# Weights of the second mixer split ahead of time, during the first MLP

## The chip, the cores and the metric

The kernel runs on one core of one Trainium2 chip. The metric is the device time of one execution in microseconds, the median of several runs. A core has TensorE (matrix products, with loads of the stationary operand listed apart), VectorE, ScalarE, GpSimd, and SyncE, which here issues nearly all DMAs. In the profile they are PE and PEld, DVE, ACT, POOL and SP. Each engine takes its own instructions in order and waits on semaphores for the others.

## The reference

The reference is one step of a decoder trunk of two layers in float32, for 1024 prompt tokens and 8 decode tokens together (T = 1032 columns), with a model dimension of 1024. Layer 0 has a hybrid mixer (gated delta rule and retention), layer 1 a Mamba-2 state-space mixer; each is followed by a squared-ReLU MLP with 4096 hidden features:

```python
h = rms_norm(x, norm_mix[layer])
out = mixer(h)                       # hybrid_mixer, then ssd_mixer
x = x + out
h = rms_norm(x, norm_mlp[layer])
x = x + einsum('blf,fd->bld', relu(einsum('bld,df->blf', h, w1)) ** 2, w2)
```

The second mixer starts with one projection of the normalised tokens:

```python
proj = einsum('bld,de->ble', h, w_in)          # w_in [1024, 5152]
z, xbc, dt_raw = split_last(proj, SSM_IN_SIZES)  # 2048, 3072, 32 columns
xbc = silu(causal_conv(xbc, conv_w, conv_b))
```

then runs a chunked scan over the tokens in four groups of heads, gates the result with silu(z), normalises it by group, and projects it back. The norm's weight per feature, norm_mix[1], can be multiplied into the rows of w_in; the norm's factor per token is applied to the product.

## The kernel before

**Exact parts.** A float32 product is made of three faster products. Each operand is split into two exact parts, a high one, which is the operand rounded by a cast to the type float32r, and a low one, the operand minus the high part. `mm3` (lines 148 to 152) adds whi·xhi, whi·xlo and wlo·xhi into one PSUM bank. The residual stream lies in SBUF as eight pairs of tiles xh, xl of [128, 1032]. Tokens are taken in three pieces of 344 columns.

**Weights.** `load_w` (lines 132 to 146) prepares 128 x 512 weights: a DMA on SyncE's queue brings them into a tile `raw` (three buffers, L136); GpSimd multiplies them by the norm's weight where there is one (L140); ScalarE casts the high part (L144); VectorE, or GpSimd for the down and output projections, subtracts to get the low part (L145). The parts have six buffers `hl`, that is three pairs. `load_half` calls it for half of an m-tile (128 output features by 512 of the 1024 inputs).

**Projections.** `products` (lines 165 to 175) makes an m-tile: for each of the two halves, three pieces of tokens by four k-tiles by three products, 36 products on one pair of parts. `gemm_units` evicts the three PSUM banks by a function that the caller gives. `gemm_flush` (lines 207 to 222) multiplies a block of up to eight k-tiles into all eight m-tiles of the model dimension.

**First MLP.** `mlp` (lines 1210 to 1325) makes 32 hidden m-tiles with `up`; after every fourth, `down` adds the block before into the residual's eight accumulators. `up` evicts through VectorE, ScalarE and GpSimd (L1225 to L1228), `down` by one VectorE addition (L1236).

**Second mixer.** Its 40 m-tiles of w_in lie in memory as `wis`, ten to a group of heads: four of x, one of B, one of C, four of the gate z. `ssm_setup` makes the narrow projection of dt and the first m-tile (number 4). In `ssm_mixers`, `conv_tile` and `gate` make the others; their evictions are L1451 (into the convolution's input sxc) and L1476 (into z). Between them runs `ssd_group`, the scan of a group: decays E (L1621 to L1629), the tokens scaled by dt, xdt (L1600), the scores sc (L1613), the state S, and the decode step with its state tiles dS (L1710 to L1731). The output projection's first block starts while the last group ends.

**Order.** The code emits the pieces of scan and projections in turn; a planner then sets each engine's order from these priorities, its own cost model and the buffers that are free at its modelled time. So a load is issued well before the product that needs it, but on each engine the order is fixed, and an instruction that waits holds all that stand behind it. On SyncE's queue the weight loads stand between the loads of the decode states (L1710), of the convolution states (L1458) and the stores of the new ones (L1468, L1469).

Of the kernel before, what the change touches and what calls it, by code (L numbers as in the profile page):

```python
# [18 lines left out]
P = 128  # L19
T = 1032                     # 1024 prompt tokens, then 8 decode tokens  # L20
# [4 lines left out]
KT = 8                       # k-tiles of the model dimension  # L25
WN = 384                     # tokens of a group of a narrow projection
CH = 128                     # mixer chunk
# the tokens in nines of 128, the last of which overlaps
# [3 lines left out]
HID = 32                     # hidden m-tiles of the MLP  # L32
PAST = 8192

# columns of the packed per-feature vectors
# [9 lines left out]
# order of the hybrid projection's m-tiles (first column of each)  # L45
# [14 lines left out]
# blocks of the output projections: the first packed column's k-tile, the mixer outputs  # L60
# [4 lines left out]
BS = 8                       # diagonal blocks that are inverted row by row  # L65
MASK_STEPS = [8, 16]         # doubling steps on whole chunks, with masks
BLOCK_STEPS = [32, 64]       # and on the blocks themselves
# [6 lines left out]
# columns of the retention's constants  # L74
# [9 lines left out]
class Pools:  # L84
    """A mixer's two pools: what the output projection's first block needs or reuses, and the rest."""
# [10 lines left out]
class Kern:  # L96
# [35 lines left out]
    def load_w(self, src, n, normw=None, lo_eng=None, dst=None, norm_eng=None):  # L132
        """src [128, n] of a packed weight unit -> exact float32r high and low parts."""
# [19 lines left out]

    def load_half(self, src, kh, M, normw):
        return self.load_w(src[:, kh * 4 * M:(kh + 1) * 4 * M], 4 * M, normw[:, kh * 4:kh * 4 + 4])

    def narrow(self, ps, w, x, k):
        """A k-tile of a projection of M <= 32 columns, in float32: ps[32 n:32 n + M, i] its token WN * n + i; the
        array takes the three groups of tokens side by side."""
        M = w.shape[1]  # L160
        for n in range(3):
            c = slice(n * WN, min(T, n * WN + WN))
            self.nc.tensor.matmul(ps[32 * n:32 * n + M, 0:c.stop - c.start], lhsT=w, rhs=x[:, c], start=k == 0, stop=k == KT - 1)

    def products(self, src, M, normw, pss):
        """The products of an m-tile over the model dimension; yields after every sixth."""
# [10 lines left out]
    def others(self):  # L177
        """The banks of the small products, for an m-tile."""
        return [self.pm(), self.ps2(), self.ps2()]

    def gemm_units(self, src, M, normw, evict, other=False):
        """One m-tile over the model dimension; evict(n, psum [M, 344]). other: in the banks of the small products.

        Yields after every sixth of the products; a pending rstd is worked out between them. self.first: the
        tile's psum, where its products are there already."""
# [21 lines left out]
    def gemm_flush(self, src, parts, evict):  # L207
        """A block of k-tiles into all 8 m-tiles; src(m) the packed weights [128, 128 * k-tiles]."""
# [16 lines left out]
    def split_piece(self, m, n, src, ssq, tp):  # L225
        """src [128, 344] fp32 becomes the residual's piece (m, n); its squares go to ssq."""
# [16 lines left out]
    def rsqrt(self, out, src):  # L243
        """out = (src) ** -0.5 for a small tile."""
# [7 lines left out]
    def rstd_from(self):  # L252
        """rstd_bc[:, t] = (sum_p ssq[p, t] / 1024 + eps) ** -0.5 on every partition; ssq lies where rstd_bc does."""
# [22 lines left out]
    def spread_end(self, pb, r, n):  # L276
        """pb[p, i] = r[128 - n + i] on every partition."""
        self.nc.tensor.matmul(pb[:, 0:n], lhsT=r.to_broadcast([P, P]), rhs=self.ident[:, P - n:P], start=True, stop=True)

    def spread(self, pb, rs):  # L280
        """pb[p, c * 128 + i] = rs[i, c] on every partition, from rs's two exact float32r parts."""
# [14 lines left out]
    def load_x(self, gp):  # L296
        """The tokens, as exact parts; their rstd; and the narrow projection, not yet scaled by it."""
# [25 lines left out]
        def square(m):  # L323
            """x[m]'s squares; those of four tiles are added up."""
# [49 lines left out]
    def softplus(self, out, x, tp, tag, bufs=None):  # L374
        """log1p(exp(x)) = max(x, 0) + 2 atanh(u / (2 + u)), u = exp(-|x|)."""
# [19 lines left out]
    def conv_silu(self, out, xc, st, wcol, bcol, tp):  # L395
        """Depthwise causal conv over the tokens of one 128-feature tile, then silu.

        xc [128, 3 + 1032] has three zero columns ahead; st [128, 3, 8] the decode rows;
        wcol(i) the tap halved, bcol the bias halved (or None)."""
# [16 lines left out]
    def silu2(self, x, scale, tp):  # L416
        """x (1 + tanh(scale x)) in place, in two halves."""
# [39 lines left out]
    def load_mixed(self, k, raw, hi, lo):  # L457
        """A spilled mixer output [128, 1024] and its decode columns, as exact parts."""
# [7 lines left out]
    def out_first(self, name, c0, parts, stage):  # L466
        """The first k-tiles of an output projection, with the residual, go to memory."""
# [12 lines left out]
    def hyb_mixers(self, gp):  # L480
# [34 lines left out]
        def ret(t, rr, vv, gg):  # L515
            for i in range(2):
# [3 lines left out]
                for q in range(4):          # the halves of each head's features change places  # L520
# [25 lines left out]
        def step():  # L546
            """Emits a sixth of a projection (and the end of the one before)."""
# [6 lines left out]
        def project(n):  # L554
            """Emits the projections up to tile n."""
# [6 lines left out]
        def weave(mix, need, rate):  # L562
            """Emits a mixer's pieces with `rate` sixths of a projection after each."""
# [16 lines left out]
        # the output projection's first block fills in while the last mixers finish  # L580
# [22 lines left out]
    def gdn_setup(self, gp, ba):  # L603
# [14 lines left out]
        gnh = gp.tile([P, 5], F32, name="gnh")     # norm weights of the gated outputs, halved  # L618
# [4 lines left out]
        # beta and decay: [8, T] -> token-major [128, 9, 8]  # L623
# [35 lines left out]
        # rows of the cumulated decay, as exact float32r parts stacked on the contraction  # L659
# [19 lines left out]
    def gdn_head(self, gp, h, feat, st):  # L679
# [10 lines left out]
        def bc(x, n=4):      # [128, n] -> [128, n, 128]  # L690
            return x.unsqueeze(2).to_broadcast([P, n, 128])

        def b3(x, n=4):      # [128, 128] -> [128, n, 128]
# [7 lines left out]
        for bi in range(2):  # L701
# [33 lines left out]
            # decay, transposed: DT[j, c, i] = exp(min(G_i - G_j, mask))  # L735
# [19 lines left out]
            # the diagonal blocks of the transposed factor, [block's row, chunk, row i]  # L755
# [5 lines left out]
        # their inverses: every row of a block needs the block's entries, lb[p, chunk, i, k] = L[block of p, i, k]  # L761
# [24 lines left out]
        # X = (I + L)^-1 by block doubling, two chunks at a time; XT its transpose  # L786
        units = [(B[bi], slice(2 * i, 2 * i + 2)) for bi in range(2) for i in range(2)]
        # (a step changes the columns of each 2b-block's upper right quarter alone, from its first b columns of X)
        for b in MASK_STEPS:
            def q4(x, half):      # [128, 2, 128] -> [128, 2, blocks, b], a half of each block's columns  # L790
                return x.rearrange("p c (n t b) -> p c n t b", t=2, b=b)[:, :, :, half, :]

            def c4(x):            # [128, 128] psum columns -> [128, 2, blocks, b]
# [60 lines left out]
        # the recurrence over the chunks  # L854
# [933 lines left out]
def pack(inp):  # L1788
# [3 lines left out]
    d = {}  # L1792
# [93 lines left out]
```

## Time and profile before

| | |
|---|---|
| runs | 3256.97, 3253.94, 3255.11 us; median 3255.11 |
| span of the profiled execution, first to last instruction | 3239.5 us |
| that execution's own time | not shown apart from its span |
| busy: TensorE, VectorE, ScalarE, GpSimd | 3086.4, 1740.3, 896.2, 1241.3 us |
| DMA | 202.13 MB, mean 62 GB/s |

A row of a group reads: line, engine, operation, output<-inputs by the program's names, shapes, count | busy time, mean ns of one | idle time of the engine just before them, and what ended it. A row of a window reads: start and end, length, then the busy time and count of PE, PEld, DVE, ACT and POOL, the clock that TensorE was granted (1.00 is full), the busy share of the DMA engines and GB/s. In a row of waits the instruction on the left waited for the one on the right. Matmuls overlap in the pipeline, so a single one's length is not its distance to the next.

### The profile page before, as it was taken

To read this page: it belongs to the slowest core of one execution; us is meant where nothing else is said; L and a number is where in the kernel's file an instruction comes from. 1 tells how busy PE (TensorE), PEld (TensorE's weight loads), DVE (VectorE), ACT (ScalarE), POOL (GpSimd) and SP (SyncE) were. 2 spreads that over 40 slices of the span, in tenths; PEclk is the share of its full clock that TensorE was granted. 3 is DMA by queue.
4 is the path that set the end of the run, shared out by engine and by line. 5 is a ranking of instruction groups with operands and counts; after the bars stand their busy time and mean duration, and the time that the engine had idled before them with its cause. 6 is when DMAs were issued, how large, how long until landed. Compare 5 with 4: busy or idle time off the path is not lost. (4 is left out here: it accounts for less than half of the span.)

```text
span 3239.5 us, 49390 instructions
## 1 busy us (share of the span) xinstructions
PE 3086.4 (95%) x19566; PEld 2929.6 (90%) x19566; DVE 1740.3 (54%) x3201; ACT 896.2 (28%) x1828; POOL 1241.3 (38%) x1234
## 2 busy tenths in 40 slices
PE   7989998989999999999999999999899999999998
PEld 6888888879999999999987788887899999999998
DVE  7664667464333333337886785967635333333334
ACT  3222221223111111114444444354213111111112
POOL 4232324155333323225355555444625332332324
PEclk9899999889999999999998898998899999999999
DMA  3011103142111111111111111222431111111112
GB/s 123 20 47 54 47 26 112 55 168 64 46 46 47 49 46 46 48 48 40 55 56 58 69 62 43 82 69 79 157 140 43 46 47 49 46 46 50 46 46 72
DMA packets 102326, 202.13 MB, mean 62 GB/s; under 512 B 12624, under 2 KB 27728, under 8 KB 102096
## 3 DMA queue, kind: packets, MB, share of 16 engines
q1 hardware_dynamic: 94800, 173.82, 16.7%
q0 software_dynamic: 7296, 25.17, 2.0%
q8 instruction: 154, 2.52, 0.3%
q14 instruction: 76, 0.62, 0.1%
HBM read 157.94 MB, written 38.89 MB: 61 GB/s over the span
## 5 line engine op out<-in xcount | busy, mean ns | idle before, releaser
L150 PE MATMUL pg<-xh,whi 128*128 128x344 f32 x3072 | 1020.7, 332 | 10.2 <-DVE sxc L1451 6.5
L152 PE MATMUL pg<-xh,wlo 128*128 128x344 f32 x3072 | 1012.9, 330 | 2.8 <-DVE wlo L145 2.8
L151 PE MATMUL pg<-xl,whi 128*128 128x344 f32 x3072 | 1009.0, 328 | 0.0
L150 PEld LDWEIGHTS pg<-xh,whi 128*128 128x128 f32 x3072 | 593.0, 193 | 27.7 <-issue 8.8
L152 PEld LDWEIGHTS pg<-xh,wlo 128*128 128x128 f32 x3072 | 592.8, 193 | 12.7 <-issue 5.2
L144 ACT CAST whi<-raw 128x512 fp32r<-128x512 f32 (+2 forms) x443 | 271.0, 612 | 1191.5 <-PE pg L151 723.9
L151 PEld LDWEIGHTS pg<-xl,whi 128*128 128x128 f32 x3072 | 592.3, 193 | 8.8 <-issue 5.8
L140 POOL TENSOR_TENSOR raw<-raw,vec 128x512 f32<-128x512 f32 x264 | 300.7, 1139 | 589.9 <-DMA raw<-w 339.7
L151 PE MATMUL pg<-alo,whi 128*128 128x344 f32 (+2 forms) x1476 | 472.4, 320 | 0.0
L152 PE MATMUL pg<-ahi,wlo 128*128 128x344 f32 (+2 forms) x1476 | 472.3, 320 | 0.0
L150 PE MATMUL pg<-ahi,whi 128*128 128x344 f32 (+2 forms) x1476 | 471.6, 319 | 0.0
L1236 DVE TENSOR_TENSOR acc<-acc,pg 128x344 f32<-128x344 f32 x360 | 182.8, 511 | 385.4 <-PE pg L152 385.4
L145 POOL TENSOR_TENSOR wlo<-raw,whi 128x512 fp32r<-128x512 f32 (+2 forms) x179 | 223.7, 1251 | 327.7 <-ACT whi L144 326.6
L145 DVE TENSOR_TENSOR wlo<-raw,whi 128x512 fp32r<-128x512 f32 x264 | 209.6, 794 | 193.3 <-ACT whi L144 172.2
L1227 POOL TENSOR_TENSOR r<-r 128x344 f32<-128x344 f32 x192 | 145.9, 760 | 387.6 <-ACT ahi L1226 338.5
L152 PEld LDWEIGHTS pg<-ahi,wlo 128*128 128x128 f32 x1476 | 277.6, 188 | 0.0
L150 PEld LDWEIGHTS pg<-ahi,whi 128*128 128x128 f32 x1476 | 277.5, 188 | 0.0
L151 PEld LDWEIGHTS pg<-alo,whi 128*128 128x128 f32 x1476 | 277.3, 188 | 0.0
L1228 DVE TENSOR_TENSOR alo<-r,ahi 128x344 fp32r<-128x344 f32 x192 | 135.6, 707 | 253.8 <-POOL r L1227 253.8
L1226 ACT ACTIVATE ahi<-r 128x344 fp32r<-128x344 f32 x192 | 94.5, 492 | 338.5 <-DVE r L1225 338.5
L1225 DVE SCALAR_TENSOR_TENSOR r<-pg,rstd_bc 128x344 f32<-128x344 f32 x186 | 94.8, 510 | 76.9 <-PE pg L152 75.6
L150 PE MATMUL pg<-mhi,whi 128*128 128x344 f32 x408 | 131.3, 322 | 4.1 <-DVE acc L1342 4.1
(534 smaller groups left out, 4422.9 us busy)
## 6 DMA issues: line engine op xcount, KB each, us to landing
raw<-w SPq DMA_DIRECT2D x256, 256.0 KB, 2.6
raw<-wis SPq DMA_DIRECT2D x80, 256.0 KB, 2.6
raw<-wih SPq DMA_DIRECT2D x56, 256.0 KB, 2.6
mraw<-spill SPq DMA_DIRECT2D x17, 512.0 KB, 4.1
accd<-ost SPq DMA_DIRECT2D x48, 172.0 KB, 2.1
acc<-accd SPq DMA_DIRECT2D x16, 516.0 KB, 6.9
dS<-sstate SPq DMA_DIRECT2D x32, 256.0 KB, 3.5
o_sssm<-dS POOLq DMA_DIRECT2D x32, 256.0 KB, 2.4
```

The source lines that it names most:

```text
L140: (norm_eng or nc.gpsimd).tensor_tensor(out=r3, in0=r3, in1=normw.unsqueeze(2).to_broadcast([P, k, n // k]), op=ALU.mult)
L144: nc.scalar.copy(hi[:, :n], raw[:, :n])
L145: (lo_eng or nc.vector).tensor_tensor(out=lo[:, :n], in0=raw[:, :n], in1=hi[:, :n].bitcast(F32), op=ALU.subtract)
L150: t.matmul(ps, lhsT=whi, rhs=xhi, start=start, stop=False)
L151: t.matmul(ps, lhsT=whi, rhs=xlo, start=False, stop=False)
L152: t.matmul(ps, lhsT=wlo, rhs=xhi, start=False, stop=stop)
L1225: nc.vector.scalar_tensor_tensor(out=r, in0=ps, scalar=0.0, in1=self.rstd_bc[:, s], op0=ALU.max, op1=ALU.mult)
L1226: nc.scalar.activation(hi[:, s], r, AF.Square)
L1227: nc.gpsimd.tensor_tensor(out=r, in0=r, in1=r, op=ALU.mult)
L1228: nc.vector.tensor_tensor(out=lo[:, s], in0=r, in1=hi[:, s].bitcast(F32), op=ALU.subtract)
L1236: nc.vector.tensor_tensor(out=s, in0=s, in1=ps, op=ALU.add)
```

## The change

A new generator `presplit` walks through the second mixer's 80 weight halves. For each it loads the weights into a tile of its own, multiplies by the norm's weight on GpSimd, casts on ScalarE and subtracts on VectorE, the same arithmetic as before, and stores both parts in a scratch buffer in device memory (40 tiles of [128, 4, 512], 1 MB each). The first MLP takes one step of it after each `up` and after the first seven m-tiles of each `down`, so all 80 are emitted before the last `down`. The second mixer passes the m-tile's number instead of its weights, and `load_half` then loads the two parts from the scratch buffer straight into an `hl` pair. The dt projection's weights (`wdt`), the other projections and the second MLP are as before. The MLP's pool holds six more tiles of 2 KB per partition. Comments are also taken out of the file, which shifts line numbers.

```diff
+    def presplit(self, tp):
+        nc, I = self.nc, self.I
+        normw = self.V("mix1", 0, 8)
+        for i in range(40):
+            for kh in range(2):
+                raw = tp.tile([P, 512], F32, tag="praw", name="praw", bufs=2)
+                nc.sync.dma_start(raw, I["wis"][i][:, kh * 512:kh * 512 + 512])
+                r3 = raw.rearrange("p (k c) -> p k c", k=4)
+                nc.gpsimd.tensor_tensor(out=r3, in0=r3, in1=normw[:, kh * 4:kh * 4 + 4].unsqueeze(2).to_broadcast([P, 4, 128]), op=ALU.mult)
+                hi, lo = [tp.tile([P, 512], F32R, tag="phl", name=nm, bufs=4) for nm in ("phi", "plo")]
+                nc.scalar.copy(hi, raw)
+                nc.vector.tensor_tensor(out=lo, in0=raw, in1=hi.bitcast(F32), op=ALU.subtract)
+                for s, x in enumerate((hi, lo)):
+                    nc.sync.dma_start(self.split[i][:, kh * 2 + s], x.bitcast(F32))
+                yield
+
     def load_half(self, src, kh, M, normw):
+        if isinstance(src, int):
+            hl = [self.wp.tile([P, 512], F32R, tag="hl", name=nm, bufs=6) for nm in ("whi", "wlo")]
+            for s, x in enumerate(hl):
+                self.nc.sync.dma_start(x.bitcast(F32), self.split[src][:, kh * 2 + s])
+            return hl
...
+            pre = iter(()) if last else self.presplit(tp)
             def up(t):
...
                 self.gemm_tile(I["w1"][l, t], 128, normw, ev, t == 1)
+                next(pre, None)
             def down(b):
...
-                for _ in self.gemm_flush(lambda m: I["w2"][l, b, m], [parts.pop(k) for k in ks], ev):
-                    pass
+                for m, _ in enumerate(self.gemm_flush(lambda m: I["w2"][l, b, m], [parts.pop(k) for k in ks], ev)):
+                    if m < 7:
+                        next(pre, None)
...
                 down(HID // 4 - 1)
+                for _ in pre:
+                    pass
...
-        for u, _ in enumerate(self.products(I["wis"][4], 128, normw, self.first)):
+        for u, _ in enumerate(self.products(4, 128, normw, self.first)):
...
-            self.gemm_tile(I["wis"][ti // 4 * 10 + ti % 4 if ti < 16 else ti % 4 * 10 + ti // 4], 128, normw, ev)
+            self.gemm_tile(ti // 4 * 10 + ti % 4 if ti < 16 else ti % 4 * 10 + ti // 4, 128, normw, ev)
...
-            self.gemm_tile(I["wis"][g * 10 + 6 + i], 128, normw, ev)
+            self.gemm_tile(g * 10 + 6 + i, 128, normw, ev)
...
+        sp = ctx.enter_context(tc.tile_pool(name="split", bufs=1, space=bass.MemoryType.DRAM))
+        k.split = [sp.tile([P, 4, 512], F32, name=f"split{i}") for i in range(40)]
```

## The prediction

> **What bounds the kernel now.** I read the page first, for engine shares and the slices in time; then two windows, the second mixer's projections (1489 to 2270 us) and the first MLP (790 to 1480 us).
>
> ```profile
> span 3239.5 us, 49390 instructions
> PE 3086.4 (95%) x19566; PEld 2929.6 (90%) x19566; DVE 1740.3 (54%) x3201; ACT 896.2 (28%) x1828; POOL 1241.3 (38%) x1234
> ```
> ```profile
> core 0: us, PE busy (x) PEld busy (x) DVE busy (x) ACT busy (x) POOL busy (x), PEclk, DMA share, GB/s
> 1489.00:2270.00 781.00, 731.26 (x4406) 650.22 (x4405) 597.71 (x955) 347.66 (x792) 379.63 (x341) 0.92 0.18 63
> 790.00:1480.00 690.00, 690.00 (x4387) 690.00 (x4386) 245.59 (x438) 130.03 (x236) 217.85 (x219) 1.00 0.15 47
> ```
>
> TensorE is the bound everywhere, but the two stages differ. In the MLP it has no idle time and the full clock, and every other engine is under 36% busy. In the mixer it is idle for 781 - 731.3 = 49.7 us, and its granted clock is 0.92, which costs about 731.3 x 0.08 = 58.5 us. So 108 us is the most that the mixer can give. VectorE there is 77% busy. The next view is who waits there (1480 to 2290 us); the numbers are the total in us, how often, and the longest.
>
> ```profile
> PE pm L1621 <- DVE xdt L1600: 14.0, 8, 3.0
> PE pm L1621 <- DVE sc L1613: 13.0, 5, 3.4
> PE pg L150 <- DVE sxc L1451: 6.5, 4, 2.7
> ...
> PE pg L152 <- DVE wlo L145: 2.8, 4, 1.7
> PE ps L1648 <- DVE x L1650: 2.2, 3, 1.0
> ...
> PE pg L150 <- ACT whi L144: 1.3, 2, 0.7
> ```
>
> Almost all of TensorE's idle time ends with a VectorE instruction. Here is one of the eight waits for xdt, with VectorE's instructions ahead of it (start, duration).
>
> ```profile
> 1640.23 0.50 PE L1621 MATMUL pm<-sgrow,ssel 64*128 64x256 f32 x2 [2.73 <-DVE xdt L1600]
> ```
> ```profile
> 1636.36 1.78 DVE L145 TENSOR_TENSOR wlo<-raw,whi 128x512 fp32r<-128x512 f32 x1
> 1638.06 0.67 DVE L1731 TENSOR_REDUCE dy<-dpr 128x4 f32<-128x512 f32 x1
> 1638.66 0.92 DVE L1451 TENSOR_TENSOR sxc<-pg,rstd_bc 128x344 f32<-128x344 f32 x2
> 1639.51 0.68 DVE L1600 TENSOR_TENSOR xdt<-pm,dt 128x512 f32<-128x512 f32 x1
> ```
>
> VectorE works without a pause, and the weights' subtraction (L145) stands in that queue. In the timeline all eight waits for xdt, and the three for x at L1650, have an L145 in the run-up like this one.
>
> **What the change removes from the mixer.** Each of its 80 weight halves loses three instructions.
>
> ```profile
> L140 POOL TENSOR_TENSOR raw<-raw,vec 128x512 f32<-128x512 f32 x80 | 98.3, 1229 | 134.3 <-DMA raw<-wis 104.5 <-DVE sxc L1451 12.4 <-DVE z L1476 10.0
> L145 DVE TENSOR_TENSOR wlo<-raw,whi 128x512 fp32r<-128x512 f32 x80 | 78.6, 983 | 13.3 <-PE pg L152 11.8 <-ACT whi L144 1.2
> ...
> L144 ACT CAST whi<-raw 128x512 fp32r<-128x512 f32 x85 | 52.6, 619 | 99.1 <-PE pg L151 41.6 <-issue 30.8 <-POOL raw L140 13.3
> ```
>
> Busy time falls by 98 us on GpSimd, 79 on VectorE (598 to about 519), and 80 x 0.619 = 50 on ScalarE. None of that is path time itself; what counts is the idle of TensorE behind it.
> - Waits for xdt, 14.0 us: each has one L145 of mean 0.98 us in front, so 8 x 0.98 = 7.9 us goes. Bounds: 0, if the next instruction in the queue has to wait for something else anyway, and 14.0. I take 7.9, since the queue shown has no idle in it.
> - Waits for x at L1650, 2.2 us over three: L145 is longer than the mean wait of 0.73, so all 2.2.
> - Waits for wlo and whi, 2.8 + 1.3 = 4.1 us: the instructions are gone; a late DMA could take their place (below). I take 4.1.
> - The waits for sc (13.0), sxc (6.5) and the others stay.
>
> That is 14.2 us of idle time, out of 20.3 in these groups. The second term is the clock. These are six stretches of low clock in the mixer that start with or just behind such a wait, and, last, one that starts with the longest wait for sc (3.4 us). The columns are those of the windows above:
>
> ```profile
> 1640.00:1646.00 6.00, 5.76 (x21) 4.21 (x21) 6.00 (x8) 4.33 (x14) 4.03 (x3) 0.72 0.01 4
> 1678.00:1690.00 12.00, 11.52 (x44) 9.04 (x45) 10.74 (x14) 9.48 (x25) 5.57 (x6) 0.72 0.09 32
> 1742.00:1758.00 16.00, 15.19 (x54) 12.95 (x55) 8.62 (x11) 9.21 (x25) 9.63 (x6) 0.57 0.13 48
> 1782.00:1794.00 12.00, 11.35 (x40) 9.61 (x41) 7.23 (x8) 9.52 (x26) 7.14 (x6) 0.58 0.08 23
> 2170.00:2178.00 8.00, 8.00 (x49) 7.00 (x48) 2.55 (x4) 4.65 (x10) 2.48 (x1) 0.79 0.01 2
> 2238.00:2246.00 8.00, 7.51 (x32) 6.01 (x32) 5.31 (x9) 5.97 (x17) 3.49 (x3) 0.79 0.29 98
> 1998.00:2022.00 24.00, 21.10 (x82) 18.29 (x84) 11.70 (x20) 9.50 (x23) 11.57 (x10) 0.57 0.09 33
> ```
> The second stretch starts with this wait:
>
> ```profile
> 1678.48 0.50 PE L1621 MATMUL pm<-sgrow,ssel 64*128 64x256 f32 x2 [1.98 <-DVE xdt L1600]
> ```
>
> Busy time x (1 - clock) of the first six is 1.6 + 3.2 + 6.5 + 4.8 + 1.7 + 1.6 = 19.4 us. I let as much of it go as of the idle that starts it, 14.2 / 20.3 = 0.70: 13.6 us (bounds 0 and 19.4).
>
> The Trainium skill ("TensorE: Matmul & The Clock Gate", section "Why this matters for your kernels") says that the clock falls back when TensorE idles for more than about 3 us between bursts. By that rule no wait that L145 lengthens is long enough, the second term is 0, and the time is 3240.9; this trace disagrees, since 1.98 us of idle at 1678.48 stands ahead of 12 us at 0.72.
>
> **What it adds to the first MLP.** Eighty units of one load (L140's kind of 256 KB), one GpSimd multiplication, one ScalarE cast, one VectorE subtraction, two stores of 256 KB. The first row prices a load, the second is the nearest to a store; the third is the time SyncE takes for an issue.
>
> ```profile
> raw<-wis SPq DMA_DIRECT2D x80, 256.0 KB, 2.6
> ...
> o_sssm<-dS POOLq DMA_DIRECT2D x32, 256.0 KB, 2.4
> ```
> ```profile
> L136 SPq DMA_DIRECT2D raw<-w x256: 327/328/377, 758.9 to 3181.4; - x128
> ```
> ```profile
> L140 POOL TENSOR_TENSOR raw<-raw,vec 128x512 f32<-128x512 f32 x57 | 60.3, 1057 | 168.3 <-DMA raw<-w 163.9 <-DVE acc L1236 4.4
> ```
> ```profile
> L144 ACT CAST whi<-raw 128x512 fp32r<-128x512 f32 x122 | 75.7, 620 | 385.5 <-PE pg L151 204.8 <-PE pg L152 136.3 <-POOL raw L140 40.6
> ```
> ```profile
> L145 DVE TENSOR_TENSOR wlo<-raw,whi x79: 669/692/2412, 1498.6 to 2264.3; 128x512 fp32r<-128x512 f32 x79
> ```
>
> GpSimd gets 80 x 1.057 = 85 us (218 to 303 of 690), ScalarE 80 x 0.62 = 50 (130 to 180), VectorE 80 x 0.69 = 55, at worst 80 x 2.41 = 193 (246 to 301, at most 439). SyncE issues 240 more DMAs, 240 x 0.328 = 79 us; they move 80 x 3 x 256 KB = 63 MB, some 91 GB/s on top of the 47. TensorE's uninterrupted 690 us hide all of it: cost 0. Without that cover the three instructions of a unit would be 2.37 us on the path, 190 us in all.
>
> The store is where a wait is added: SyncE waits for the cast, then for the subtraction, and the MLP's own weight loads (L136) are queued behind it; GpSimd's and ScalarE's weight work waits for those, and TensorE for that. The cast L144 shows the slack: of 385.5 us idle before it, 341 ended when TensorE released a buffer, so weights sit ready, three halves ahead. A half lasts 36 products; the MLP's 4387 in 690 us make 5.7 us. A store must hold SyncE for more than two halves, 11 us, before TensorE feels it; lower bound 0, upper bound one such miss at each of the eight down projections, about 3 us each, 24 us. I take 0.
>
> **What is moved.** The mixer's 80 loads become 160, straight into the product's buffers: 160 x 0.328 = 52 us of SyncE's 781. The wait for a free buffer moves from ScalarE (41.6 us on L144) to SyncE; the raw data no longer waits ahead of it. Cost 0 if the three pairs of buffers suffice.
>
> Sum: 14.2 + 13.6 = 27.8 us, 0.85%. The profiled span of 3239.5 becomes 3211.7. No time of that execution beside its span is shown; the median of the runs, 3255.1, lies 15.6 above it, which I leave as it is: 3255.1 - 27.8 = 3227.3.
>
> **The rivals.**
> - *More comes free.* GpSimd stood 104.5 us in front of L140 until a load landed, with all its later work behind it, and L140 overlaps VectorE's work (L145 itself goes from 0.69 to 2.41). Against: the worst waits, for sc, follow five L1727 with no L140 beside them. If half of what is left goes, (108 - 28) / 2 = 40 us more: 3187. On the overlap, the Trainium skill ("GPSIMD Engine Reference", section "Specifications") has the two engines share their SBUF interfaces when VectorE reads two SBUF inputs; L145's spread agrees.
> - *The clock stays low.* The idle goes but the low stretches come all the same, as at 1998 where L145 has no part: 3255.1 - 14.2 = 3240.9. This is the time by the rule above.
> - *The waits only change place.* TensorE reaches the next dependency earlier and waits there, for sc or sxc; the idle total stays at 50: 3255. For it speaks that 13.0 + 6.5 us already end so. Against it, VectorE gets 13% less to do.
> - *Late weights (slower).* SyncE takes its DMAs in order, and now only three pairs stand ahead:
>
> ```profile
> SPq L1468 <- POOL sco L1453: 20.3, 4, 7.4
> ...
> SPq L1458 <- DVE bc L413: 16.1, 3, 5.7
> ```
>
> At a change of group a store (L1468) and a load (L1458) hold it for up to 7.4 + 5.7 = 13.1 us. A pair then costs 2 x 0.33 + 2.6 = 3.3 us, and two pairs of cover are 11.4 us, so it decides from 8.1 us on. Each miss costs 3.3 us and a low stretch of some 5 us (the mean of those above is 3 to 9). Two in each of four groups: 8 x 8 = 64, less 28: 3291. Against it: over the whole mixer a half lasts 781 / 80 = 9.8 us, which makes the cover 19.
>
> **How the numbers follow.** Forecast 0.43; more comes free 0.20; the clock stays 0.10; only a change of place 0.12; late weights, in the mixer or the MLP, 0.15. A measurement of this kernel tells 0.2%, 6.5 us. Faster is 0.43 + 0.20 + 0.10 = 0.73, same 0.12, slower 0.15. The forecast's own range is from 19.4 + 20.3 = 39.7 us of gain to 4.1: 3215 to 3251. The whole range reaches to 3187 below and, above, over the case of no change to 3262: outside are most of the late weights and a few in a hundred below.
>
> **What would show it.** Right: the MLP's window keeps 690 us of busy TensorE at 1.00 with GpSimd near 303; in the mixer VectorE falls by 79 us or more, waits for xdt fall from 14.0 to about 6, and the clock rises to 0.93 or 0.94. Wrong: a wait of TensorE for a DMA of whi or wlo; idle in the MLP; or xdt, sc and sxc that still add up to 33 us.

## The result: 1.3% slower

The changed kernel takes 3294.72 us (median of 4 runs, 3292.54 to 3309.71), against 3254.53 (3253.21 to 3256.97) for the kernel before in the same session. The ratio is 1.0132, with a 95% interval of 1.0108 to 1.0157. The forecast was 3227.

The page after, first and second part (the rows of engines, then TensorE's clock and the DMA share in 40 slices of 82.3 us):

```profile
span 3291.4 us, 49967 instructions
...
PE 3106.3 (94%) x19566; PEld 2939.0 (89%) x19566; DVE 1710.0 (52%) x3201; ACT 897.8 (27%) x1828; POOL 1237.5 (38%) x1234
...
PEclk9899999899899999999998899898999999999999
DMA  3011103144777311111232232232441111111112
```

The DMA row shows where to look: three slices at 0.7, some 820 to 1070 us, which the kernel before doesn't have. To compare stages I cut both traces at events that both have: the first MLP's first eviction `r`, the mixer's first `sxc`, and the last load of `acc` in the mixer's output projection. The windows of the kernel before, first MLP, then mixer:

```profile
787.00:1524.00 737.00, 735.28 (x4676) 732.74 (x4676) 278.63 (x497) 150.44 (x282) 248.77 (x251) 1.00 0.15 47
1524.00:2354.00 830.00, 766.92 (x4581) 685.67 (x4579) 626.90 (x986) 354.22 (x786) 411.90 (x364) 0.92 0.21 73
```

The same two of the changed kernel, and then the first 320 us and the next 450 us of its MLP:

```profile
794.00:1605.00 811.00, 759.52 (x4678) 747.30 (x4677) 336.61 (x571) 191.00 (x356) 329.58 (x323) 0.98 0.38 119
1605.00:2405.00 800.00, 756.68 (x4578) 675.94 (x4577) 535.00 (x908) 312.87 (x710) 324.37 (x290) 0.93 0.32 101
790.00:1110.00 320.00, 267.21 (x1542) 256.93 (x1543) 154.53 (x239) 89.15 (x163) 165.97 (x157) 0.94 0.73 230
1110.00:1560.00 450.00, 450.00 (x2862) 450.00 (x2861) 159.12 (x285) 85.47 (x155) 141.49 (x142) 1.00 0.16 47
```

The mixer gains 30 us: TensorE's idle time falls from 63.1 to 43.3, and its busy time by 10.2. The MLP loses 74: idle time rises from 1.7 to 51.5, and the same number of products takes 24.2 us longer, of which 0.02 x 759.5, about 15, is the clock. The rest, some 9, is about what the ends of the waits take. In a run of products one starts 0.157 us after the other, because they overlap; the last product before a wait counts with its whole 0.33 us, and from the first behind it to the next it is 0.29. At the 31 waits over 0.1 us that is (0.17 + 0.13) x 31 = 9. So a wait costs some 0.3 us more than the idle time that the profile shows for it. All of the loss lies before 1110 us. After that the MLP runs as before, 450 busy of 450.

Why it ends there is told by SyncE's rows in the changed kernel: the first and last issue of the units' loads, and the MLP's own weight loads from 780 to 1086 us and from 780 to 1600 us.

```profile
L161 SPq DMA_DIRECT2D praw<-wis x80: 357/396/1331, 781.3 to 1085.2; - x80
...
L136 SPq DMA_DIRECT2D raw<-w x40: 328/333/669, 780.9 to 1082.2; - x40
...
L136 SPq DMA_DIRECT2D raw<-w x123: 327/328/669, 780.9 to 1555.3; - x123
```

The code emits a unit after every step of the MLP, but all 80 run among the first 40 of 123 weight loads, one every 3.8 us. The next rows are the waits of the changed kernel from 790 to 1560 us, by the engine that waits (total in us, how often, longest):

```profile
PE pg L150 <- DVE r L1249: 38.7, 15, 5.1
PE pg L150 <- DVE acc L1261: 12.5, 15, 2.6
...
POOL praw L163 <- DMA praw<-wis: 97.8, 54, 7.4
...
ACT phi L165 <- POOL praw L163: 177.9, 69, 6.2
...
DVE plo L166 <- ACT phi L165: 116.3, 50, 5.5
...
SPq L168 <- ACT phi L165: 117.3, 68, 4.9
SPq L168 <- DVE plo L166: 47.9, 69, 2.2
```

TensorE never waits for weights here. It waits for evictions, that is for a PSUM bank. Nor do the MLP's own weights come later than before: from 780 to 1560 us GpSimd waits 111.0 us for them in the changed kernel, at most 5.8 at a time, and 163.9, at most 5.7, in the kernel before. One case from the timeline of the changed kernel (start, duration, and in brackets the idle time before and its releaser):

```profile
822.37 0.39 PE L150 MATMUL pg<-xh,whi 128*128 128x344 f32 x1 [3.55 <-DVE r L1249]
...
825.91 1.04 POOL L163 TENSOR_TENSOR praw<-praw,vec 128x512 f32<-128x512 f32 x1 [3.22 <-DMA praw<-wis]
826.99 0.62 ACT L165 CAST phi<-praw 128x512 fp32r<-128x512 f32 x1 [6.19 <-POOL praw L163]
...
827.64 0.69 DVE L166 TENSOR_TENSOR plo<-praw,phi 128x512 fp32r<-128x512 f32 x1 [5.41 <-ACT phi L165]
...
828.98 1.34 DVE L1252 TENSOR_TENSOR alo<-r,ahi 128x344 fp32r<-128x344 f32 x1 [0.65 <-POOL r L1251]
...
830.24 0.50 DVE L1249 SCALAR_TENSOR_TENSOR r<-pg,rstd_bc 128x344 f32<-128x344 f32 x1
...
830.80 0.66 PE L150 MATMUL pg<-xh,whi 128*128 128x344 f32 x1 [5.14 <-DVE r L1249]
```

Read it from the load: GpSimd stands until a unit's weights land, ScalarE's cast until GpSimd is done, VectorE's subtraction until the cast. The MLP's own subtraction alo and the eviction r stand behind that subtraction in VectorE's order, and TensorE behind r, 5.14 us. ScalarE's cast also holds up the MLP's ahi, which runs at 827.51, right behind it; GpSimd's r (L1251), for which alo waits another 0.65 us, needs that ahi. SyncE, with the store of phi next in its queue, issued nothing between 823.01 and 827.63.

### The profile page after: what moved, and what is told of

Same layout as the page of the kernel before. It is cut to its first block, busy times and chain, and to the rows that moved or that the text cites. A ratio compares the mean times of both kernels' runs of the same rounds, so it can differ in the third digit from the quotient of the medians.

```text
span 3291.4 us, 49967 instructions
## 1 busy us (share of the span) xinstructions
PE 3106.3 (94%) x19566; PEld 2939.0 (89%) x19566; DVE 1710.0 (52%) x3201; ACT 897.8 (27%) x1828; POOL 1237.5 (38%) x1234
## 5 line engine op out<-in xcount | busy, mean ns | idle before, releaser
L144 ACT CAST whi<-raw 128x512 fp32r<-128x512 f32 (+1 forms) x363 | 221.7, 611 | 956.9 <-PE pg L151 606.3
L140 POOL TENSOR_TENSOR raw<-raw,vec 128x512 f32<-128x512 f32 x184 | 203.7, 1108 | 412.4 <-DMA raw<-w 283.7
L145 POOL TENSOR_TENSOR wlo<-raw,whi 128x512 fp32r<-128x512 f32 (+2 forms) x179 | 226.7, 1268 | 303.0 <-ACT whi L144 302.9
L1251 POOL TENSOR_TENSOR r<-r 128x344 f32<-128x344 f32 x192 | 148.2, 772 | 333.7 <-ACT ahi L1250 291.3
L1252 DVE TENSOR_TENSOR alo<-r,ahi 128x344 fp32r<-128x344 f32 x192 | 144.3, 752 | 246.1 <-POOL r L1251 246.1
L145 DVE TENSOR_TENSOR wlo<-raw,whi 128x512 fp32r<-128x512 f32 x184 | 134.6, 731 | 149.6 <-ACT whi L144 141.5
L152 PE MATMUL pg<-mhi,wlo 128*128 128x344 f32 x408 | 131.2, 322 | 1.7 <-POOL wlo L145 1.7
```

The source lines that it names most:

```text
L140: (norm_eng or nc.gpsimd).tensor_tensor(out=r3, in0=r3, in1=normw.unsqueeze(2).to_broadcast([P, k, n // k]), op=ALU.mult)
L144: nc.scalar.copy(hi[:, :n], raw[:, :n])
L145: (lo_eng or nc.vector).tensor_tensor(out=lo[:, :n], in0=raw[:, :n], in1=hi[:, :n].bitcast(F32), op=ALU.subtract)
L152: t.matmul(ps, lhsT=wlo, rhs=xhi, start=False, stop=stop)
L1251: nc.gpsimd.tensor_tensor(out=r, in0=r, in1=r, op=ALU.mult)
L1252: nc.vector.tensor_tensor(out=lo[:, s], in0=r, in1=hi[:, s].bitcast(F32), op=ALU.subtract)
```

## Experiments

The stages of each kernel's profiled execution, from the start times of the three events above; "rest" is from the last load of `acc` to the end of the span. Ratios are to the kernel before, timed in the same session.

| kernel | time, us | ratio (95%) | start of MLP | MLP | mixer | rest |
|---|---|---|---|---|---|---|
| before | 3254.53 | 1 | 786.9 | 737.4 | 829.5 | 885.7 |
| the change | 3294.72 | 1.0132 (1.0108–1.0157) | 793.5 | 811.4 | 800.1 | 886.4 |
| split ahead, old mixer | 3342.99 | 1.0253 (1.0216–1.0290) | 813.1 | 814.2 | 825.3 | 885.8 |
| new mixer, no splitting | 3228.72 | 0.9898 (0.9870–0.9926) | 807.9 | 736.8 | 800.9 | 884.4 |
| traffic only | 3280.46 | 1.0078 (1.0049–1.0106) | 808.1 | 770.5 | 816.2 | 883.9 |
| subtraction on GpSimd | 3327.71 | 1.0206 (1.0165–1.0247) | 817.0 | 829.5 | 801.3 | 883.9 |
| shared buffers | 3258.00 | 1.0012 (0.9993–1.0031) | 819.2 | 763.8 | 790.3 | 884.3 |
| one raw buffer | 3344.78 | 1.0280 (1.0240–1.0319) | 808.3 | 852.8 | 793.2 | 885.7 |
| deeper buffers | 3310.01 | 1.0173 (1.0133–1.0213) | 813.6 | 815.3 | 797.8 | 885.7 |
| no multiplication | 3272.77 | 1.0064 (1.0045–1.0083) | 802.0 | 780.7 | 802.5 | 883.5 |
| held units | 3239.71 | 0.9954 (0.9937–0.9971) | 806.6 | 741.3 | 797.5 | 884.4 |
| load ahead, not held | 3302.63 | 1.0171 (1.0130–1.0211) | 809.6 | 813.0 | 794.6 | 885.4 |
| held, load late | 3333.54 | 1.0266 (1.0217–1.0315) | 810.4 | 842.3 | 792.5 | 884.3 |

The start of the MLP varies from 787 to 819 us although the change touches nothing before it. So causes are read from the MLP and mixer columns, and spans are not compared across kernels. Each row is one execution. That of the kernel before adds up to 3239.5 us, 15 less than its median time. Its MLP, which is full of work at a clock of 1.00, leaves no room for that, but the other columns may. The mixer's column also shows how far a stage moves without a change of its code: 816 to 830 us with the old mixer, 790 to 803 with the new one. A difference of some 10 us between two rows of that column is therefore not read. The MLP's column repeats better: 737.4 and 736.8 without the splitting.

### The two halves of the change by themselves

Split ahead, but the mixer prepares its weights as before:

```diff
...
-        self.gemm_tile(g * 10 + 6 + i, 128, normw, ev)
+        self.gemm_tile(I["wis"][g * 10 + 6 + i], 128, normw, ev)
```

> The splitting during the first MLP is kept, with its loads and stores, but the second mixer loads and splits its weights itself as before, so the stored parts are not used. All theories: if the first MLP's loss (its first eviction to the mixer's first convolution input went from 752 to 823 us, +71) belongs to the splitting alone, the time is 3254 + 75 = about 3330 and the mixer's stretch is as before. If part of the loss came from the mixer's changed loads being hoisted into the MLP, the time is under 3315.

The new mixer with only two units split; every m-tile of its projection uses the first one's weights, so that the loads stay and the splitting goes:

```diff
-        for i in range(40):
+        for i in range(1):
...
-    self.nc.sync.dma_start(x.bitcast(F32), self.split[src][:, kh * 2 + s])
+    self.nc.sync.dma_start(x.bitcast(F32), self.split[0][:, kh * 2 + s])
```

> Only the first m-tile is split in the MLP (2 units of 80); the mixer loads parts straight into the product's buffers, always those of the first m-tile, so every m-tile of its projection uses the first one's weights. This is the mixer's half of the change alone. Theory that the mixer gained what was predicted (28 us) and the MLP lost the rest: 3254 - 28 = 3227, TensorE without idle in the MLP. Rival, that the mixer's gain came from the shifted schedule by chance: 3245 to 3265.

The halves are nearly independent: MLP 814.2 with the splitting and 736.8 without it, mixer 825.3 with old loading and 800.9 with new. By time, 2.53% is lost and 1.02% gained. The mixer's part of the forecast holds (by time 32 us with the new mixer alone, forecast 28); the question is the MLP's 74 us.

### Traffic, and the subtraction's engine

Each unit only loads 256 KB and stores it twice; no engine works on it, and the mixer is the old one:

```diff
-                nc.gpsimd.tensor_tensor(out=r3, in0=r3, in1=..., op=ALU.mult)
...
-                for s, x in enumerate((hi, lo)):
-                    nc.sync.dma_start(self.split[i][:, kh * 2 + s], x.bitcast(F32))
+                for s in range(2):
+                    nc.sync.dma_start(self.split[i][:, kh * 2 + s], raw)
```

> The MLP only moves data: each of the 80 units loads 256 KB and stores it twice, with no multiplication, cast or subtraction; the mixer is as before. Theory A (order: subtractions and casts of the splitting stand in the engines' fixed order ahead of evictions and wait there): 3255 +- 6. Theory B (traffic: the DMA engines, 0.73 busy in that stretch, bring the MLP's weights late): 3310 to 3330, with TensorE waiting for whi or wlo. Theory C (the arithmetic itself, engines in each other's way): 3255.

The MLP still loses 33 us; by the ratio of the times it is 25, which none of the three expectations gave. These are waits on SyncE, GpSimd, VectorE and TensorE (780 to 1680 us):

```profile
SPq L161 <- DMA split<-praw: 94.3, 80, 3.0
SPq L164 <- DMA praw<-wis: 73.1, 74, 3.6
...
POOL raw L140 <- DMA raw<-w: 229.5, 61, 14.0
...
DVE alo L1248 <- POOL r L1247: 160.8, 95, 12.5
...
PE pg L150 <- DVE r L1245: 22.2, 4, 8.7
```

Here SyncE is the engine that stands: a unit's load waits until the stores out of its buffer have landed, the stores wait for their load, and the MLP's weight loads wait behind both. GpSimd then stands up to 14.0 us for a weight load (before, 5.7 at most), VectorE up to 12.5 behind GpSimd (before, 1.9), and TensorE behind VectorE. Four waits for `r` make 22 of the 33 us. So this loss, too, is one of waiting in order; whether slower transfers add to it, this kernel does not tell.

Next, the subtraction of the change moves from VectorE to GpSimd:

```diff
-                nc.vector.tensor_tensor(out=lo, in0=raw, in1=hi.bitcast(F32), op=ALU.subtract)
+                nc.gpsimd.tensor_tensor(out=lo, in0=raw, in1=hi.bitcast(F32), op=ALU.subtract)
```

> The whole change, with the splitting's subtraction on GpSimd instead of VectorE, so that it no longer stands between VectorE's evictions. Theory A (order): TensorE's waits for r and acc, 51 us in the MLP, fall under 15 and the time to 3235 to 3250. Theory B (traffic): as the changed kernel, 3295. Theory C (engines' work): GpSimd gets 80 x 1.29 = 103 us more in that stretch, where it is busy 166 of 320 us; 3295 to 3330.

That VectorE's place in the chain alone is the cause falls: without the subtraction there, the MLP loses 92 us. The wait moves with it: VectorE's own `alo` now waits for GpSimd's `r`, 6.5 us at the longest, where the change has 2.6. But GpSimd also has more work, 425 us of the MLP against 330, and 3327.71 lies in the range that was expected if the engines' work is the price (3295 to 3330). So this kernel does not separate waiting from work.

```profile
DVE alo L1252 <- POOL r L1251: 173.0, 94, 6.5
```

### Buffers and the amount of work

The units in the buffers of the MLP's own weights, by the same helper:

```diff
-                raw = tp.tile([P, 512], F32, tag="praw", name="praw", bufs=2)
...
-                nc.vector.tensor_tensor(out=lo, in0=raw, in1=hi.bitcast(F32), op=ALU.subtract)
+                hi, lo = self.load_w(I["wis"][i][:, kh * 512:kh * 512 + 512], 512, normw[:, kh * 4:kh * 4 + 4])
```

> The whole change, but the splitting takes its tiles from the buffers of the MLP's own weights, so the planner can't run it ahead of them: on SyncE's queue the 80 units stand among 116 of the MLP's 128 weight loads, in the changed kernel among 40. Theory D (density: 80 units packed into the first 320 us lock the engines' fixed orders to the loads' landing): the MLP loses under 10 us, the mixer gains its 32 us: 3222 to 3235. Theory E (every unit costs TensorE its share wherever it stands, 75 us / 80 = 0.9 us each): 3290 to 3300. Rival F (three pairs are too few to share: the MLP's own weights come late): TensorE waits for wlo or whi in the MLP, 3260 or more.

```profile
L162 SPq DMA_DIRECT2D split<-wlo x80: 326/379/423, 807.6 to 1498.5; - x80
```

With shared buffers the units can't run ahead of the MLP: their stores, above, spread over 691 us, and the loss falls to 26 us. TensorE's waits in the MLP are again for evictions (9.9 us for r, 8.2 for acc), with 1.8 us for a wlo, so scarce weights are not what is left. The whole is no different from before (1.0012, an interval with 1 in it); 3222 to 3235 was expected if density is the cause, 3290 or more if each unit has its price, and it is neither.

One raw buffer in place of two; and, in another kernel, three raw and six part buffers:

```diff
-                raw = tp.tile([P, 512], F32, tag="praw", name="praw", bufs=2)
+                raw = tp.tile([P, 512], F32, tag="praw", name="praw", bufs=1)
```

```diff
-                raw = tp.tile([P, 512], F32, tag="praw", name="praw", bufs=2)
+                raw = tp.tile([P, 512], F32, tag="praw", name="praw", bufs=3)
...
-                hi, lo = [tp.tile([P, 512], F32R, tag="phl", name=nm, bufs=4) for nm in ("phi", "plo")]
+                hi, lo = [tp.tile([P, 512], F32R, tag="phl", name=nm, bufs=6) for nm in ("phi", "plo")]
```

> The whole change with one load buffer instead of two for the splitting; the 80 units then stand among 79 weight loads instead of 40. Theory D (density): about half of the MLP's 75 us is lost, 3245 to 3265. Theory E (each unit costs its share): 3290 to 3300.

> The whole change with three load buffers and three pairs of part buffers for the splitting, instead of two and two; 80 units among 44 weight loads, the density of the changed kernel. If a late load (GpSimd waits 98 us for it in the MLP) is what holds the engines, a third buffer takes about half of the loss: 3255 to 3270. If the packed work or the traffic itself does it: 3285 to 3300.

The loads with one buffer, GpSimd's wait for them and VectorE's for the cast:

```profile
L161 SPq DMA_DIRECT2D praw<-wis x80: 333/386/1737, 797.7 to 1364.7; - x80
...
POOL praw L163 <- DMA praw<-wis: 200.8, 61, 5.9
...
DVE plo L166 <- ACT phi L165: 259.5, 59, 5.7
```

One buffer nearly halves the density, to a unit every 7.1 us, and the loss grows to 115 us. So density by itself is not what is paid: there are fewer units in a time, but each waits longer. Neither expectation had this, since the one put the loss at half and the other left it as it was. Deeper buffers do not help (MLP 815.3; the time is above what was expected for either theory).

The change without the multiplication by the norm's weight, which leaves the weights of the mixer's projection unscaled:

```diff
-                nc.gpsimd.tensor_tensor(out=r3, in0=r3, in1=..., op=ALU.mult)
```

> The whole change without the multiplication by the norm's weight on GpSimd (the weights of the mixer's projection are split unscaled); 80 units among 45 weight loads. Theory G (GpSimd is the link: its multiplication waits for the load, and the MLP's squares stand behind it, and VectorE behind those): the loss falls to what traffic alone costs, 25 us, so 3240 to 3252. If VectorE's subtraction behind ScalarE's cast is enough by itself: 3275 to 3300.

A chain shorter by one engine loses 43 us in place of 74. The time, 3272.77, lies between the two ranges that were expected. The MLP's loss fits a price of the chain's length, but also one of GpSimd's work, so it does not decide.

### Holding the units back

The theory that was left: the planner puts each unit where its modelled time has room, the unit depends on nothing but its own buffers, so all are pulled ahead; and their instructions then stand in four fixed orders until real loads land. The test keeps every load, store and operation, but issues the load one unit ahead and makes the multiplication depend on the MLP's latest product:

```diff
-                raw = tp.tile([P, 512], F32, tag="praw", name="praw", bufs=2)
-                nc.sync.dma_start(raw, I["wis"][i][:, kh * 512:kh * 512 + 512])
+                raw, nxt = nxt, load(2 * i + kh + 1) if 2 * i + kh < 79 else None
...
+                nw = tp.tile([P, 4], F32, tag="pnw", name="pnw", bufs=2)
+                nc.vector.scalar_tensor_tensor(out=nw, in0=self.dep, scalar=0.0, in1=normw[:, kh * 4:kh * 4 + 4], op0=ALU.mult, op1=ALU.add)
-                nc.gpsimd.tensor_tensor(out=r3, in0=r3, in1=normw..., op=ALU.mult)
+                nc.gpsimd.tensor_tensor(out=r3, in0=r3, in1=nw..., op=ALU.mult)
...
                 self.gemm_tile(I["w1"][l, t], 128, normw, ev, t == 1)
+                self.dep = lo.bitcast(F32)[:, T - 4:T]
                 next(pre, None)
...
                     if m < 7:
+                        self.dep = acc[m][:, T - 4:T]
                         next(pre, None)
```

> The change with each unit held back: the load of a unit is issued one unit ahead, and its multiplication needs a 128x4 copy of the norm weights that VectorE makes from the product that has just been finished, so that a unit can't be placed ahead of the MLP's own progress, and finds its weights landed. All work and all traffic of the change stay, with 80 tiny VectorE operations more. Theory H (a unit's instructions were placed at a modelled landing time and stand in the fixed orders of GpSimd, ScalarE, VectorE and SyncE until the real, later load; evictions behind them hold the PSUM banks): GpSimd's waits for the unit's load, 97.8 us after the change, fall below 15 us, the MLP stage comes to 737 to 755 us (811 with the change), the mixer stays at 800, and the time is 3225 to 3243 beside 3254 before. Traffic (the 80 loads and 160 stores themselves slow the MLP's weight loads): the 33 us of the traffic alone stay, MLP 770 or more, 3258 or more. Engines' work (one more multiplication, copy and subtraction per unit is too much for the three engines): MLP near 811, 3295.

The time is 3239.71 us against 3256.09, ratio 0.9954 (0.9937 to 0.9971): by its ratio faster than both kernels. The windows of MLP and mixer with held units, the issues of their loads, and VectorE's wait for the cast:

```profile
807.00:1548.00 741.00, 736.88 (x4677) 732.60 (x4677) 355.53 (x654) 196.20 (x358) 322.59 (x324) 1.00 0.42 132
1548.00:2345.00 797.00, 751.76 (x4579) 671.41 (x4577) 536.09 (x908) 311.95 (x710) 323.01 (x290) 0.94 0.32 101
...
L160 SPq DMA_DIRECT2D praw<-wis x80: 332/399/1984, 795.5 to 1448.2; - x80
...
DVE plo L173 <- ACT phi L172: 110.3, 80, 1.9
```

GpSimd's wait for the unit's load is gone, and the MLP costs 3.9 us more than before, with more VectorE work than the change (355.5 us against 336.6) and the same traffic. So neither traffic nor the engines' work is the price. VectorE's wait for the cast adds up to nearly the same, 110.3 us against 116.3; but no single wait is over 1.9 us where the change has up to 5.5. So short waits cost next to nothing, even at every unit. The longest wait alone does not set the price either: without the multiplication it is 5.7 us for 43 us of loss, with one raw buffer 5.7 us for 115. How many waits are long counts too.

Two kernels take the two halves of this apart. The load issued ahead, without the hold:

```diff
-                raw = tp.tile([P, 512], F32, tag="praw", name="praw", bufs=2)
-                nc.sync.dma_start(raw, I["wis"][i][:, kh * 512:kh * 512 + 512])
+                raw, nxt = nxt, load(2 * i + kh + 1) if 2 * i + kh < 79 else None
...
```

> The change with the load of each unit issued one unit ahead, but nothing that holds the unit back. Theory H: the units still run as densely as their two buffers let them, the load that is issued ahead starts only when the unit two before has been split, and GpSimd still stands for it; MLP 785 to 825 us, time 3270 to 3310. If a load issued ahead is all that was needed, the waits for it go without the hold: MLP under 755, time under 3245.

MLP 813.0: a load issued ahead is worth nothing as long as the units are as dense as before (GpSimd again waits 100.0 us for it). And the hold, but at the load, so that the unit's engines stand for its whole landing:

```diff
                 raw = tp.tile([P, 512], F32, tag="praw", name="praw", bufs=2)
+                nc.vector.tensor_copy(raw[:, 0:4], self.dep)
                 nc.sync.dma_start(raw, I["wis"][i][:, kh * 512:kh * 512 + 512])
...
```

> The change with each unit held back as in the kernel with held units, but at another place: VectorE first copies 128x4 of the product that has just been finished into the raw tile, so that the load itself starts no earlier than the product, and the multiplication, the copy and the subtraction stand behind it for the whole of its landing. Pacing, traffic and arithmetic are those of the held units (MLP 741 us); only the wait for the landing comes back. Theory H, waiting in the order is the price: GpSimd waits 80 x about 3 us for the unit's load, VectorE stands as long ahead of the next evictions, and of the 74 us 15 to 45 come back: MLP 756 to 786, time 3255 to 3285. Theory P, what the held units cured was the density (80 units at 4 us each in the first 320 us) and a wait by itself is harmless: MLP 741 to 750, time 3238 to 3250.

The window of this kernel's MLP, and its waits (780 to 1640 us):

```profile
810.00:1653.00 843.00, 769.60 (x4679) 734.56 (x4680) 350.85 (x655) 187.06 (x358) 323.81 (x325) 1.00 0.36 117
...
POOL praw L164 <- DMA praw<-wis: 216.7, 66, 5.9
...
DVE plo L167 <- ACT phi L166: 306.8, 80, 5.9
...
PE pg L150 <- DVE r L1250: 37.4, 56, 2.1
PE pg L150 <- DVE acc L1263: 30.7, 36, 1.8
```

Units spread as widely, less DMA share than with held units (0.36 against 0.42), fewer GB/s, and yet 101 us more, 1.26 us for each unit. I had expected 15 to 45 of the 74 back; it came out slower than the change itself. The wait of a unit was expected at about 3 us and is 306.8 / 80 = 3.8; how much of it reaches TensorE was put far too low. The rival, that density alone is the price, falls. SyncE waits at the held loads too (84.6 us), which this kernel does not separate; but TensorE's waits are again for evictions; for a weight it waits once, 1.7 us (held units 1.3).

TensorE's idle time is some 72 us of the loss. The other 34 are busy time (769.6 against 735.3) at a clock of 1.00. Most of that is again the ends of the waits: there are 109 over 0.1 us, the last product before one counts 0.32 us and the first behind it 0.25, where the distance in a run is 0.157. That is (0.16 + 0.10) x 109 = 28 us.

## Why the prediction was wrong

**The mixer: right in the sum.** Forecast 27.8 us, measured 829.5 - 800.1 = 29.4. Other rows of the table with the same mixer code would give 14 to 39, so an agreement to 2 us says less than it seems; the new mixer alone gained 32 us by time. TensorE's waits there in the changed kernel (1560 to 2360 us):

```profile
PE pm L1649 <- DVE sc L1641: 12.6, 5, 3.7
PE pm L1649 <- DVE xdt L1628: 7.5, 9, 2.3
PE pg L150 <- DVE sxc L1479: 5.3, 2, 2.7
...
PE ps L1688 <- DVE x L1678: 1.0, 2, 0.7
```

- xdt: 14.0 to 7.5, a gain of 6.5, forecast 7.9. The forecast read the one queue that it shows, without idle; in three of the eight, those before 1782.65, 1970.39 and 2161.81, VectorE stood 0.76 us between the subtraction and xdt, which takes up part of what goes. x: 2.2 to 1.0, forecast 0. wlo and whi: 4.1 to none, as forecast; no wait for the two loads took their place. sc and sxc stay about, as forecast. These make 6.5 + 1.2 + 4.1 = 11.8 of the 14.2.
- All idle time in the stage fell by 19.8, not 14.2: sc and sxc give 1.6, and the other 6.4 lie in smaller groups that I did not count. The clock's term, 13.6, was too large: busy time fell by 10.2 with the granted clock going from 0.92 to 0.93. Not all of that need be clock: the waits over 0.1 us fall from 45 to 29, and at 0.3 us for the ends of each that is some 5 us, an estimate from the MLP's waits. The two errors, idle too low and clock too high, nearly cancel, so the close sum is partly luck.
- The Trainium skill ("TensorE: Matmul & The Clock Gate", section "Why this matters for your kernels") puts the fall of the clock behind idle of more than about 3 us. By that the second term would be 0, and the mixer's clock rose by 0.01 nevertheless. The changed MLP has a case that agrees, 0.59 behind the wait of 3.55 us at 822.37; in the kernel with held units and a late load there is one that does not, 0.55 from 902.5 to 904 us behind a wait of 1.83.

```profile
822.30:826.00 3.70, 3.29 (x12) 2.88 (x12) 0.00 (x0) 0.00 (x0) 0.48 (x2) 0.59 0.87 233
```

**The first MLP: wrong.** The step that failed is "TensorE's uninterrupted 690 us hide all of it: cost 0". It costs 74 us, 50 of them idle time of TensorE in the MLP, which the prediction had named as a sign of being wrong. Three things in that step did not hold.
- It counted busy time. The engines did have room: GpSimd ended at 329.6 us of 811. What was missing was room in the order. The units' instructions stand among the evictions, and one that waits 5 us holds the evictions behind it, whatever share of the stage its engine is idle. The same work and the same transfers, held back and loaded a unit ahead, cost 3.9 us.
- It spread the 240 DMAs over 690 us ("some 91 GB/s on top of the 47"). They ran in 304 us, at 230 GB/s in all, and the units' loads took 4.0 us to land, not the 2.6 of the row I used:

```profile
raw<-w SPq DMA_DIRECT2D x256, 256.0 KB, 2.6
praw<-wis SPq DMA_DIRECT2D x80, 256.0 KB, 4.0
split<-phi SPq DMA_DIRECT2D x80, 256.0 KB, 3.2
```

- The one wait it looked for was the store on SyncE, with the weights as what comes late, and a bound of 24 us. That wait exists (117.3 + 47.9 us), but TensorE does not wait for weights behind it. The waits that decide are those of the unit on GpSimd, ScalarE and VectorE, which the prediction priced only by duration. Its 190 us "without that cover" was no bound of theirs either; it would be the right kind of number for what was paid, 74 / 80 = 0.92 us a unit, if one knew which part is uncovered.

**The rivals.** Late weights gave 3291, and 3294.7 was measured; the sign's chance was 0.15. But its mechanism, loads held up on SyncE in the mixer, did not occur: no wait for whi or wlo is in the mixer's list. So the rival was near by accident. "The waits only change place" came nearest in kind, but it looked for the new place in the mixer.

What would have shown the loss beforehand: to a planner that goes by modelled times and free buffers, a unit that depends on nothing else, with buffers of its own, has no reason to stay where the code emits it. With two raw buffers and 80 units it had to be asked how early they can go, and what then stands behind each instruction that needs the landing. The Trainium skill ("Perfetto Trace Analysis", section "Tensor Engine Instruction (MATMUL, LD_WEIGHTS)") says that VectorE, ScalarE and GpSimd are strict first-in first-out; the timeline at 825 us agrees, with alo and r kept behind a subtraction that waited 5.41 us.

Of the 33 us of the traffic alone, 22 are shown as waits that start from SyncE in that kernel. That this part is inside the change's 74 us, and how much, is not shown: there SyncE's orders are others.

## What to carry to other kernels

Work put into "idle" engines costs by the long waits it brings into their orders, more than by its busy time: here 80 waits of up to 1.9 us cost under 4 us, and 50 of up to 5.5 us, with what they held, 74. Ask for each added instruction what it waits for, and which eviction stands behind it. This planner pulled independent work ahead as far as its buffers went, into one dense burst; a cheap dependency on the stage's own progress, with the load issued a step earlier, turned 74 us of loss into 4. Both are needed: the load ahead without the hold left 76 us, the hold in front of the load 105.

## What was not expected of the hardware

- A VectorE operation on 128x4 can take as long as one of GpSimd. With held units the small operation pnw took 582 ns on average where it reads the accumulator:

```profile
L169 DVE SCALAR_TENSOR_TENSOR pnw<-acc,vec 128x4 f32<-128x4 f32 x49 | 28.5, 582 | 1.2
...
872.98 1.29 POOL L145 TENSOR_TENSOR wlo<-raw,whi 128x512 fp32r<-128x512 f32 x1 [3.29 <-DVE acc L1269]
872.99 1.30 DVE L169 SCALAR_TENSOR_TENSOR pnw<-acc,vec 128x4 f32<-128x4 f32 x1
```

The average is of long and short ones. Each that took over 0.3 us started just behind a GpSimd subtraction L145 that was running, and ended within 0.03 us after it, as here at 874.29; where L145 started at the same moment (within 4 ns) or later, or GpSimd did nothing, pnw took 0.16. Reading a fresh result is not the reason: right behind the subtraction that had just written `alo` it took 0.16 us too.
- The idle time of TensorE understates what a wait costs it, by 0.26 to 0.30 us for each wait here, since the products at its two ends do not overlap.
- With held units all 240 extra transfers, at 132 GB/s in the stage, cost the MLP under 4 us in all; at 230 GB/s, in the change, the same loads took 4.0 us to land instead of 3.5:

```profile
praw<-wis SPq DMA_DIRECT2D x80, 256.0 KB, 3.5
```
